# Starting the up projection on the first token half, and normalizing the second half without its weights

## The chip, the cores and the metric

One core of a Trainium2 chip runs the whole layer in one launch. The metric is the device time of that launch in microseconds, and lower is better. Before the change the median of three runs is 1382.29 us.

## The reference, cut to what matters

The layer takes 1024 tokens of width 1024. It mixes chunked attention with a gated convolution, then closes with a layer norm, and the result feeds a feed-forward block with a width of 2816 per branch:

```python
    mix = (g_att * y_att + g_conv * y_conv) @ w_o[l]
    x = layer_norm(ALPHA * x + mix, ln1_g[l], ln1_b[l])
    ffn = conv_ffn(x, w_up[l], ffn_conv_w[l], ffn_conv_b[l], w_down[l])
    x = layer_norm(ALPHA * x + ffn, ln2_g[l], ln2_b[l])

def conv_ffn(x, w_up, w_dw, b_dw, w_down):
    u = x @ w_up
    a, b = jnp.split(u, 2, axis=-1)
    a = causal_dwconv(a, w_dw, b_dw)
    return (jax.nn.gelu(a) * b) @ w_down

def layer_norm(x, g, b):
    ...
    y = xc * lax.rsqrt(var + LN_EPS) * g.astype(jnp.float32) + b.astype(jnp.float32)
```

The change sits between the first layer norm and the first products of `x @ w_up`.

## The kernel before, in words

**Precision.** Every float32 operand of a product is split into a high and a low part (`hi` by a copy on ScalarE, `lo` by a subtraction on VectorE), and each product takes three matmuls, high-high, high-low and low-high.

**The up projection.** It runs as 22 "quads". A quad computes two strips of 128 output features for all 1024 tokens. Tokens are split into two halves of 512 and the contraction into two halves of 512, and a Strassen-like form with seven products in place of eight is used. Each product is 4 x 3 matmuls of 128x512. The token side of the seven products are the forms `xf[1]` to `xf[7]`: forms 1 and 2 are the two contraction halves of the first 512 tokens, and forms 3 to 7 all need the second 512 tokens (form 4 is one block of them, 5, 6, 7 and 3 are differences and sums). The weight side: `wr` holds three raw blocks of a quad, for products 1, 3 and 2; `w13` serves products 5 and 7, and `w24` products 6 and 4, from sums that GpSimd makes (`prep_sums`, L809 to L812) into the tile `wt`. `parts_of` (L797, L798) splits weights; `product` (L821 to L823) issues the matmuls.

**What comes ahead of the quads.** The products with `w_o` (`mm3`, L196 to L198) give the sum that the layer norm closes, for token tiles 0 to 3 first and then 4 to 7. `close_tile` normalizes one tile of 128 tokens: `take` (L687) adds a bank to the residual with the sum accumulated, `norm` (L692 to L706) squares on ScalarE, makes the reciprocal root with a handful of small VectorE instructions, and applies weights and biases of the norm along the row with two VectorE instructions of 128x1024 (L705, L706). `turn0` transposes the first token half on TensorE (L745) and makes forms 1 and 2; `turn1` (L770 to L778) does so for the second half and makes forms 4, 5, 7, 6 and 3, all five for each of the four blocks `i`. In `turn1` forms 6 and 3 are computed by GpSimd (L773, L774). The normalized rows are also written to memory (`x1_d`, L858 and L872), since the last layer norm needs them again.

**Order.** The program is traced in the order of the code. A scheduler with a cost model then sets the order on each engine, by priority in program order among what it reckons ready; so the instructions of one engine can stand in another order than in the code, but each engine runs its own list in order. SBUF is laid out by the kernel's own `Arena`, which prefers places that were freed long ago; a tile in a place freed late waits for the last readers of what lay there.

**PSUM.** Eight banks: two `mm`, one `tp`, one `pv`, two pairs `s`. A quad uses `oa` and `od` (two `mm`, or `tp` and `pv`) and a pair for `oc` and `ob`.

Of the kernel before, what the change touches and what calls it, by code (L numbers as in the profile page):

```python
# [14 lines left out]
P = 128  # L15
T = 1024
# [25 lines left out]
C_FB = C_FW + FT * FTAPS  # L42
NPAR = C_FB + FT

# [71 lines left out]
def build(ctx, tc, xT, x, w_v, w_in, w_ao, w_co, w_o, w_up, w_dn, par, rel, rows, out):  # L116
# [561 lines left out]
    def close_tile(t, scale, g_bc, b_bc, out=None):  # L678
# [81 lines left out]

    def turn1():

        for n in (4, 5, 7, 6, 3):
            part(n)
        for i in range(4):
            o = bank2()
            turned(o[:, 0], 1, i + 4)
            turned(o[:, 1], 1, i)
            x22, x5, x7, x6, x3 = (sb(f"xs{n}_{i}", [P, HT]) for n in (4, 5, 7, 6, 3))
            S.activation(x22, o[:, 0], AF.Copy)  # L770
            V.tensor_sub(x5, o[:, 1], x22)
            V.tensor_sub(x7, xs[1][i], o[:, 1])
            G.tensor_sub(x6, x5, xs[1][i])  # L773
            G.tensor_add(x3, x6, xs[2][i])  # L774
            for n, a in ((4, x22), (5, x5), (7, x7), (6, x6), (3, x3)):
                hi, lo = xf[n][i]
                S.activation(hi, a, AF.Copy)  # L777
                V.tensor_sub(lo, a, f32(hi))  # L778
            sb.free(x22, x5, x7, x6, x3)
        sb.free(*xs[1], *xs[2])  # L780
# [18 lines left out]

    def prep_raw(q):  # L800

        if q < 2 * FP:
            parts_of(wr, quads[q][:, 1:4])

# [51 lines left out]
    x1_d = [tc.dram_tile([P, D], F32, name=f"x1_d{t}") for t in range(8)]  # L856
    for t in range(4):
        nc.sync.dma_start(x1_d[t], res[t])  # L858
        sb.free(res[t])
    for a in wo + mix[1]:  # L860
        sb.free(*a)
    sb.free(g_bc, b_bc)
    wt.append(sb("wt", [P, 4, HT]))
    w13 = pair_of_parts("w13", 2)
    w24 = pair_of_parts("w24", 2)
    prep_sums(0)
    parts_of(w13, wt[0][:, 0:2])
    parts_of(w24, wt[0][:, 2:4])
    turn1()
    quad_r.append(sb("quad1", [P, 4, HT]))  # L870
    for t in range(4, 8):
        nc.sync.dma_start(x1_d[t], res[t])  # L872
        sb.free(res[t])

    a_r = Ring("a", 2, [P, 2 + T])
    for t in a_r.t:
        G.memset(t[:, 0:2], 0.0)
    y_r = Ring("y", 4, [P, T])
    tmp = {n: sb(f"u{n}", [P, HT]) for n in ("1", "3", "U", "e", "21", "12", "22", "5", "6", "7", "8")}
# [3 lines left out]
    def quad(q, take11, dst21, dst12, dst22, over=None):  # L883

        if q % 2 == 0:
            oa, od = bank(), bank()
# [5 lines left out]
        done = over or (lambda n: None)  # L892
        product(oa, wr, 0, 1, True)
        done(1)
        S.activation(tmp["1"], oa, AF.Copy)
        product(od, wr, 1, 3, True)
        done(3)
        S.activation(tmp["3"], od, AF.Copy)
        product(oa, wr, 2, 2, False)
        done(2)  # L900
        take11(oa)
# [9 lines left out]
        done(6)  # L911
        V.tensor_add(tmp["U"], tmp["1"], ob)  # L912
        V.tensor_sub(dst12, od, tmp["U"])
# [89 lines left out]

    load_quad()
    for j in range(FP):
        f2 = (j, j + FP)
        a2 = [a_r(), a_r()]
        y2 = [y_r(), y_r()]
        quad(2 * j, lambda o: S.activation(a2[0][:, 2:2 + HT], o, AF.Copy), a2[0][:, 2 + HT:], a2[1][:, 2:2 + HT],
             a2[1][:, 2 + HT:])  # L1010
        for f, a, y in zip(f2, a2, y2):
# [11 lines left out]
        quad(2 * j + 1, lambda o: V.tensor_mul(y0[:, h0], y0[:, h0], o), tmp["21"], tmp["12"], tmp["22"],  # L1023
             over if j == FP - 1 else None)
        V.tensor_mul(y1[:, h0], y1[:, h0], tmp["12"])
# [98 lines left out]
def _layout(inputs):  # L1124
# [9 lines left out]
    def cols(v):  # L1134
# [48 lines left out]
```

## Time and profile before

| | |
|---|---|
| median of 3 runs (lowest to highest) | 1382.29 us (1380.49 to 1383.54) |
| the profiled execution's own time | 1380.95 us |
| its span in the profile | 1379.2 us |
| TensorE busy | 1334.7 us (97%) |
| VectorE busy | 977.7 us (71%) |
| ScalarE busy | 605.6 us (44%) |
| GpSimd busy | 350.6 us (25%) |

The 1.75 us between the span and the profiled execution's time lie outside the span. Busy TensorE says that a matmul was in flight, at either of its two clock levels, and not that it went at its peak; so the table alone doesn't tell how much of the span is lost.

### The profile page before, as it was taken

What the parts mean: (1) busy time and instruction counts of PE and PEld (TensorE: products, weight loads), DVE (VectorE), ACT (ScalarE), POOL (GpSimd) and SP (SyncE); (2) the same over time, 40 slices, a digit from 0 to 9 for tenths busy, and PEclk for the clock granted to TensorE, in tenths of its full rate; (3) what the DMA queues carried; (4) which work ended last, traced back from release to release, by engine and by line L of the source; (5) the groups of instructions that cost most, each with busy time, mean ns of one, the idle gap of its engine ahead of it and who ended that gap; (6) DMA issues with size and microseconds to landing.
All of it is one profiled execution on the core that took longest, in us unless ns stands there. A gap on an engine that the chain in (4) does not pass through costs nothing.

```text
span 1379.2 us, 16028 instructions
## 1 busy us (share of the span) xinstructions
PE 1334.7 (97%) x6004; PEld 1082.0 (78%) x6004; DVE 977.7 (71%) x1399; ACT 605.6 (44%) x916; POOL 350.6 (25%) x247
## 2 busy tenths in 40 slices
PE   9999999999999999999959999999999999998996
PEld 8877887887888888888737888888888878777885
DVE  5278888887799935746596565566666558997668
ACT  4346555656661137322453433334333444443453
POOL 1000000000000000000055566565555546972000
PEclk9999999999999999999969999999999999999999
DMA  7011111112101111621123323332223247753323
GB/s 268 16 46 41 40 56 41 56 51 82 47 31 46 55 37 52 223 92 51 45 62 107 108 87 115 115 115 89 103 96 103 100 173 267 263 166 93 92 84 123
DMA packets 48495, 132.29 MB, mean 96 GB/s; under 512 B 5393, under 2 KB 5529, under 8 KB 45601
## 3 DMA queue, kind: packets, MB, share of 16 engines
q1 hardware_dynamic: 48416, 131.26, 27.8%
q8 instruction: 47, 0.77, 0.2%
q14 instruction: 32, 0.25, 0.1%
HBM read 101.07 MB, written 30.17 MB: 95 GB/s over the span
## 4 chain that ended last, share of the span: by engine, by line
PE 82%; DVE 9%; ACT 3%; POOL 3%; issue 2%; DMA 1%; POOLq 0%; DVEq 0%; SPq 0%; ACTq 0%
PE mm L196 6%; PE mm L197 6%; PE mm L198 6%; PE s L196 5%; PE s L197 5%; PE s L198 5%; PE s L821 4%; PE s L822 4%; PE s L823 4%; PE mm L822 2%; PE mm L823 2%; PE mm L821 2%; PE s L1051 2%; PE s L1052 2%; PE tp L456 2%; PE s L1050 2%
## 5 line engine op out<-in xcount | busy, mean ns | idle before, releaser
L196 PE MATMUL mm<-xh,whi 128*128 128x512 f32 x384 | 157.9, 411 | 2.0 <-ACT qq L266 2.0
L414 DVE SCALAR_TENSOR_TENSOR acc<-hpad,par,acc 128x1024 f32<-128x1024 f32 x120 | 152.3, 1278 | 0.7
L198 PE MATMUL mm<-xh,wlo 128*128 128x512 f32 x384 | 151.8, 395 | 0.0
L197 PE MATMUL mm<-xl,whi 128*128 128x512 f32 x384 | 151.5, 395 | 0.0
L809 POOL TENSOR_TENSOR wt<-quad 128x512 f32<-128x512 f32 x22 | 28.3, 1288 | 467.7 <-ACT junk L696 375.9
L180 ACT ACTIVATE whi<-wraw 128x1024 fp32r<-128x1024 f32 x40 | 42.4, 1060 | 109.3 <-PE s L197 65.8
L798 DVE TENSOR_TENSOR wrl<-quad,wrh 128x1536 fp32r<-128x1536 f32 x22 | 42.7, 1942 | 60.8 <-ACT wrh L797 60.8
L198 PEld LDWEIGHTS mm<-xh,wlo 128*128 128x128 f32 x384 | 72.2, 188 | 15.1
L958 POOL TENSOR_TENSOR dn<-dn,dn 128x512 f32<-128x512 f32 x44 | 73.7, 1697 | 32.7 <-DMA actr<-act_d 14.7
L196 PEld LDWEIGHTS mm<-xh,whi 128*128 128x128 f32 x384 | 72.4, 189 | 11.9 <-ACT qq L266 2.9
L197 PEld LDWEIGHTS mm<-xl,whi 128*128 128x128 f32 x384 | 72.7, 189 | 9.2
L821 PE MATMUL s<-xfh,w24h 128*128 128x512 f32 x176 | 73.5, 418 | 2.1 <-DVE uU L912 1.9
L822 PE MATMUL s<-xfh,w24l 128*128 128x512 f32 x176 | 68.8, 391 | 0.0
L823 PE MATMUL s<-xfl,w24h 128*128 128x512 f32 x176 | 68.8, 391 | 0.0
L458 ACT ACTIVATE pth<-tp 128x512 fp32r<-128x512 f32 (+3 forms) x96 | 41.5, 433 | 54.1 <-PE tp L456 53.5
L181 DVE TENSOR_TENSOR wlo<-wraw,whi 128x1024 fp32r<-128x1024 f32 x40 | 48.7, 1219 | 23.0 <-ACT whi L180 22.8
L459 DVE TENSOR_TENSOR ptl<-tp,pth 128x512 fp32r<-128x512 f32 (+3 forms) x96 | 46.8, 488 | 18.5 <-ACT pth L458 17.9
L1014 DVE SCALAR_TENSOR_TENSOR y<-a,par,y 128x1024 f32<-128x1024 f32 x22 | 38.6, 1756 | 29.3 <-ACT y L1013 29.3
L439 ACT ACTIVATE p<-p,st 128x640 f32<-128x640 f32 (+2 forms) x64 | 44.4, 694 | 28.6 <-DVE st L437 28.0
L821 PE MATMUL mm<-xfh,wrh 128*128 128x512 f32 x132 | 52.8, 400 | 3.1 <-ACT xfh L777 3.1
L1013 ACT ACTIVATE y<-a,par 128x1024 f32<-128x1024 f32 x22 | 27.4, 1245 | 62.4 <-POOL a L914 57.5
L812 POOL TENSOR_TENSOR wt<-wt,quad 128x512 f32<-128x512 f32 x22 | 54.1, 2458 | 0.9
(567 smaller groups left out, 3842.2 us busy)
## 6 DMA issues: line engine op xcount, KB each, us to landing
quad<-in_w_up SPq DMA_DIRECT2D x22, 1024.0 KB, 5.2
actr<-act_d SPq DMA_DIRECT2D x77, 256.0 KB, 2.7
wraw<-in_w_in SPq DMA_DIRECT2D x32, 512.0 KB, 3.5
act_d<-u SPq DMA_DIRECT2D x44, 256.0 KB, 2.0
dn<-in_w_dn SPq DMA_DIRECT2D x44, 256.0 KB, 4.0
act_d<-y SPq DMA_DIRECT2D x33, 256.0 KB, 2.3
res<-in_x SPq DMA_DIRECT2D x8, 512.0 KB, 5.8
wraw<-in_w_o SPq DMA_DIRECT2D x8, 512.0 KB, 3.5
```

The lines of the kernel that those rows point to most:

```text
L181: V.tensor_sub(lo, raws[i], f32(hi))
L196: PE.matmul(o, ah, bh, start=first, stop=False)
L197: PE.matmul(o, ah, bl, start=False, stop=False)
L198: PE.matmul(o, al, bh, start=False, stop=last)
L414: V.scalar_tensor_tensor(a, hp[:, j:j + T], col(C_CW + c * TAPS + j), a, op0=OP.mult, op1=OP.add)
L439: S.activation(pt, pt, AF.Exp, bias=st[:, 0:1], scale=-1.0, accum_out=st[:, 1:2])
L459: last_lo[0] = V.tensor_sub(pl[:, :w], o[:, :w], f32(ph)[:, :w])
L812: G.tensor_add(t[:, 3], t[:, 2], b[:, 3])
L821: PE.matmul(o, wh, xh, start=go, stop=False, skip_group_check=not first)
L822: PE.matmul(o, wl, xh, start=False, stop=False, skip_group_check=not first)
L823: PE.matmul(o, wh, xl, start=False, stop=i == 3, skip_group_check=not first)
L958: G.tensor_add(dn[j][d], dn[j][d], dn[j][b])
```

## The change

The up projection's first two quads get a code path of their own, and the layer norm of the second token half is split.

- `close_plain` takes the place of `close_tile` for tiles 4 to 7. Mean and variance come from `bn_stats` and `bn_aggr` on VectorE, and ScalarE writes the normalized row without weights in one instruction. Weights and biases of the norm come in at the eviction of the transposed block in `turn1`, where they lie along partitions and so are a scale and a bias of the ScalarE copy (two more groups of columns, `C_G1` and `C_B1`, in the table of parameters). The weighted row that the end of the layer needs is made apart, by `rest` (two VectorE instructions and one write).
- Products 1 and 2 of both first quads are issued ahead of `turn1`. The second quad has raw weights of its own (`wr1`), and its load stands ahead of `turn1`.
- `turn1` makes form 4 for all blocks, then 7, 5, 6 and 3, each for all four blocks, all on VectorE; `quad_first` runs the rest of the first quad in the order of 4, 7, 5, 6, 3.
- `prep_sums(0)`, the writes of tiles 0 to 3 and the `wt` tile move ahead of tile 6 in the code.

```diff
+    def close_plain(t):
+        r, st = res[t], st_r()
+        v, y, z = (st[:, i:i + 1] for i in range(13, 16))
+        def take(o, c):
+            rc = r[:, cols[c]]
+            V.scalar_tensor_tensor(rc, rc, ALPHA, o, op0=OP.mult, op1=OP.add)
+            V.bn_stats(st[:, 6 * c:6 * c + 6], rc)
+        def norm():
+            V.bn_aggr(st[:, 12:14], st[:, 0:12])
+            S.activation(y, v, AF.Sqrt, bias=eps)
+            V.tensor_scalar(v, v, EPS, None, op0=OP.add)
+            V.reciprocal(y, y)
+            V.scalar_tensor_tensor(z, v, y, y, op0=OP.mult, op1=OP.mult)
+            V.tensor_scalar(z, z, -0.5, 1.5, op0=OP.mult, op1=OP.add)
+            V.tensor_mul(y, y, z)
+            V.scalar_tensor_tensor(z, st[:, 12:13], -1.0, y, op0=OP.mult, op1=OP.mult)
+            S.activation(r, r, AF.Identity, bias=z, scale=y)
+        def rest():
+            a = sb(f"x1r{t}", [P, D])
+            V.tensor_mul(a, r, g_bc)
+            V.tensor_add(a, a, b_bc)
+            nc.sync.dma_start(x1_d[t], a)
+            sb.free(a)
+        return take, norm, rest
...
+    def turn1(after):
+        def parts(n, i, a):
+            hi, lo = sb(f"xfh{n}{i}", [P, HT], F32R), sb(f"xfl{n}{i}", [P, HT], F32R)
+            xf.setdefault(n, []).append((hi, lo))
+            S.activation(hi, a, AF.Copy)
+            V.tensor_sub(lo, a, f32(hi))
...
         for i in range(4):
             o = bank2()
-            turned(o[:, 0], 1, i + 4)
-            turned(o[:, 1], 1, i)
-            x22, x5, x7, x6, x3 = (sb(f"xs{n}_{i}", [P, HT]) for n in (4, 5, 7, 6, 3))
-            S.activation(x22, o[:, 0], AF.Copy)
-            V.tensor_sub(x5, o[:, 1], x22)
-            V.tensor_sub(x7, xs[1][i], o[:, 1])
-            G.tensor_sub(x6, x5, xs[1][i])
-            G.tensor_add(x3, x6, xs[2][i])
-            for n, a in ((4, x22), (5, x5), (7, x7), (6, x6), (3, x3)):
-                hi, lo = xf[n][i]
-                S.activation(hi, a, AF.Copy)
-                V.tensor_sub(lo, a, f32(hi))
+            for a, b, k in ((a22[i], o[:, 0], i + 4), (a21[i], o[:, 1], i)):
+                turned(b, 1, k)
+                S.activation(a, b, AF.Identity, bias=col(C_B1 + k), scale=col(C_G1 + k))
+            parts(4, i, a22[i])
+        after()
+        for i in range(4):
+            a7 = sb(f"xs7{i}", [P, HT])
+            V.tensor_sub(a7, xs[1][i], a21[i])
+            parts(7, i, a7)
...
+        for i in range(4):
+            V.tensor_sub(a21[i], a21[i], a22[i])
+            parts(5, i, a21[i])
...
+        for i in range(4):
+            V.tensor_sub(a21[i], a21[i], xs[1][i])
+            parts(6, i, a21[i])
+        for i in range(4):
+            V.tensor_add(a21[i], a21[i], xs[2][i])
+            parts(3, i, a21[i])
...
+    rests = []
     for t in range(4, 8):
-        take, norm = close_tile(t, ALPHA, g_bc, b_bc)
+        take, norm, rest = close_plain(t)
...
         norm()
+        rests.append(rest)
...
         if t == 5:
             turn0()
+            for i in range(4):
+                nc.sync.dma_start(x1_d[i], res[i])
+                sb.free(res[i])
+            wt.append(sb("wt", [P, 4, HT]))
+            prep_sums(0)
+        if t > 4:
+            rests.pop(0)()
     for a in wo + mix[1]:
         sb.free(*a)
+    quad_r.append(sb("quad1", [P, 4, HT]))
+    load_quad()
+    w24 = pair_of_parts("w24", 2)
+    parts_of(w24, wt[0][:, 2:4])
     w13 = pair_of_parts("w13", 2)
     parts_of(w13, wt[0][:, 0:2])
-    turn1()
+    wr1 = pair_of_parts("wr1", 3)
+    prep_raw(1, wr1)
+    tmp = {n: sb(f"u{n}", [P, HT]) for n in ("1", "1b")}
+    oa = [bank(), bank()]
+    for o, w, u in ((oa[0], wr, "1"), (oa[1], wr1, "1b")):
+        product(o, w, 0, 1, True)
+        S.activation(tmp[u], o, AF.Copy)
+        product(o, w, 2, 2, False)
+
+    def after():
+        prep_sums(1)
+        rests.pop(0)()
+        for t in range(4, 8):
+            sb.free(res[t])
+        sb.free(g_bc, b_bc)
+
+    turn1(after)
...
+    def quad_first(take11, dst21, dst12, dst22):
+        od, cb = ps_t.tile([P, HT], F32, tag="tp", name="tp"), bank2()
+        oc, ob = cb[:, 0], cb[:, 1]
+        take11(oa[0])
+        product(oc, w24, 1, 4, True)
+        S.activation(tmp["3"], oc, AF.Copy)
+        product(oc, w13, 1, 7, False)
+        product(od, w13, 0, 5, True)
+        V.tensor_add(tmp["e"], tmp["3"], od)
+        parts_of(w13, wt[0][:, 0:2])
+        product(ob, w24, 0, 6, True)
+        V.tensor_add(tmp["U"], tmp["1"], ob)
+        V.tensor_add(dst21, tmp["U"], oc)
+        G.tensor_sub(dst22, tmp["e"], dst21)
+        parts_of(w24, wt[0][:, 2:4])
+        product(od, wr, 1, 3, False)
+        V.tensor_sub(dst12, od, tmp["U"])
```

The second quad runs in `quad` with its products 1 and 2 left out, since they are begun already, and with `wr1` in place of `wr`. All later quads are as before.

## Rows read from the trace of the kernel before

**Rows 1.** Windows over the hand-over: length, busy time of each engine, granted clock.

```profile
682.00:685.42 3.42, 3.42 (x17) 2.77 (x16) 1.98 (x7) 1.54 (x3) 0.00 (x0) 1.00 0.00 0
...
696.59:722.79 26.20, 20.10 (x62) 13.35 (x62) 25.36 (x29) 14.62 (x25) 11.64 (x9) 0.61 0.18 59
722.79:757.76 34.97, 31.55 (x129) 23.85 (x130) 21.88 (x19) 13.78 (x14) 19.73 (x13) 1.00 0.31 101
...
779.00:1000.00 221.00, 221.00 (x960) 178.20 (x959) 134.55 (x127) 83.06 (x86) 128.07 (x81) 1.00 0.29 103
```

**Rows 2.** Timeline of TensorE: start, duration, line, tiles, idle before and releaser.

```profile
685.42 0.60 PE L745 MATMUL s<-ident,res 128*128 128x128 f32 x4
685.77 0.48 PE L821 MATMUL mm<-xfh,wrh 128*128 128x512 f32 x1
...
696.59 2.40 PE L745 MATMUL s<-ident,res 128*128 128x128 f32 x10 [7.35 <-DVE res L706]
...
724.32 0.40 PE L822 MATMUL mm<-xfh,w13l 128*128 128x512 f32 x1
...
729.31 0.39 PE L823 MATMUL s<-xfl,w24h 128*128 128x512 f32 x1
```

**Rows 3.** Timeline of VectorE over the close of tile 7 and `turn1`.

```profile
656.61 0.14 DVE L700 TENSOR_SCALAR st<-st 128x1 f32<-128x1 f32 x1
...
657.50 1.28 DVE L706 SCALAR_TENSOR_TENSOR res<-res,st,b 128x1024 f32<-128x1024 f32 x1
...
686.00 0.67 DVE L687 SCALAR_TENSOR_TENSOR res<-res,pv 128x512 f32<-128x512 f32 x1
...
716.57 0.68 DVE L771 TENSOR_TENSOR xs<-s,xs 128x512 f32<-128x512 f32 x1
717.17 0.67 DVE L772 TENSOR_TENSOR xs<-xs,s 128x512 f32<-128x512 f32 x1
717.76 4.97 DVE L778 TENSOR_TENSOR xfl<-xs,xfh 128x512 fp32r<-128x512 f32 x5
```

**Rows 4.** Timeline of GpSimd in the same stretch.

```profile
688.48 1.27 POOL L809 TENSOR_TENSOR wt<-quad 128x512 f32<-128x512 f32 x1 [375.92 <-ACT junk L696]
...
717.39 1.29 POOL L773 TENSOR_TENSOR xs<-xs,xs 128x512 f32<-128x512 f32 x1 [3.10 <-ACT u L895]
718.76 1.62 POOL L774 TENSOR_TENSOR xs<-xs,xs 128x512 f32<-128x512 f32 x1
...
727.13 1.30 POOL L809 TENSOR_TENSOR wt<-quad 128x512 f32<-128x512 f32 x1 [4.23 <-DMA quad<-in_w_up]
```

**Rows 5.** Waits of the DMA queue: who waited for whom, total, times, longest.

```profile
SPq L790 <- DVE xfl L778: 25.3, 1, 25.3
```

**Rows 6.** Groups of instructions by line: busy us, mean ns.

```profile
L664 DVE TENSOR_TENSOR t<-t,t 128x1024 f32<-128x1024 f32 x8 | 9.8, 1221 | 0.1
L798 DVE TENSOR_TENSOR wrl<-quad,wrh 128x1536 fp32r<-128x1536 f32 x22 | 42.7, 1942 | 60.8 <-ACT wrh L797 60.8
L443 DVE TENSOR_SCALAR p<-p,st 128x512 f32<-128x512 f32 x8 | 3.9, 483 | 0.1
L1013 ACT ACTIVATE y<-a,par 128x1024 f32<-128x1024 f32 x22 | 27.4, 1245 | 62.4 <-POOL a L914 57.5 <-ACT u L895 2.8 <-DVE a L917 2.0
L797 ACT ACTIVATE w13h<-wt 128x1024 fp32r<-128x1024 f32 x22 | 23.3, 1060 | 56.2 <-PE s L823 53.1 <-POOL wt L810 3.1
L777 ACT ACTIVATE xfh<-xs 128x512 fp32r<-128x512 f32 x20 | 12.0, 626 | 6.7 <-POOL xs L774 2.6 <-POOL xs L773 2.3 <-DVE xs L771 1.7
L699 ACT ACTIVATE st<-st,eps 128x1 f32<-128x1 f32 x16 | 4.5, 290 | 2.5 <-DVE st L698 2.5
```

**Rows 7.** DMA issues by line: size, median us to landing.

```profile
quad<-in_w_up SPq DMA_DIRECT2D x22, 1024.0 KB, 5.2
...
x_d<-res SPq DMA_DIRECT2D x8, 512.0 KB, 2.6
```

More of the change, by code (lines that the diff above doesn't have):

```diff
@@ L42 @@
 C_FB = C_FW + FT * FTAPS
-NPAR = C_FB + FT
+C_G1 = C_FB + FT
+C_B1 = C_G1 + KD
+NPAR = C_B1 + KD
 FP = FT // 2
@@ L759, in turn0 @@
             S.activation(xs[n][i], tp, AF.Copy)
[L761 to L764 removed]
+    def turn1(after):
[4 more added lines that the diff above has]
+            V.tensor_sub(lo, a, f32(hi))
+        a22 = [sb(f"xs4{i}", [P, HT]) for i in range(4)]
+        a21 = [sb(f"xs5{i}", [P, HT]) for i in range(4)]
         for i in range(4):
             o = bank2()
[L767 to L779 removed]
+            for a, b, k in ((a22[i], o[:, 0], i + 4), (a21[i], o[:, 1], i)):
[7 more added lines that the diff above has]
+            parts(7, i, a7)
+            sb.free(a7)
+        for i in range(4):
+            V.tensor_sub(a21[i], a21[i], a22[i])
+            parts(5, i, a21[i])
+            sb.free(a22[i])
+        for i in range(4):
[4 more added lines that the diff above has]
+            parts(3, i, a21[i])
+            sb.free(a21[i])
         sb.free(*xs[1], *xs[2])
@@ L798, in parts_of, with prep_raw @@
         V.tensor_sub(lo, src, f32(hi))
-    def prep_raw(q):
+    def prep_raw(q, dst=None):
         if q < 2 * FP:
-            parts_of(wr, quads[q][:, 1:4])
+            parts_of(dst or wr, quads[q][:, 1:4])
     def prep_sums(q):
@@ L836, in build @@
     close_tiles((2, 3, 0, 1), lambda t: o8[2 * t:2 * t + 2], ALPHA, g_bc, b_bc)
+    x1_d = [tc.dram_tile([P, D], F32, name=f"x1_d{t}") for t in range(8)]
+    rests = []
     for t in range(4, 8):
-        take, norm = close_tile(t, ALPHA, g_bc, b_bc)
+        take, norm, rest = close_plain(t)
         for c in range(2):
@@ L877, in build, with quad @@
         G.memset(t[:, 0:2], 0.0)
-    y_r = Ring("y", 4, [P, T])
-    tmp = {n: sb(f"u{n}", [P, HT]) for n in ("1", "3", "U", "e", "21", "12", "22", "5", "6", "7", "8")}
+    y_r = Ring("y", 2, [P, T])
+    for n in ("3", "U", "e", "21", "12", "22"):
+        tmp[n] = sb(f"u{n}", [P, HT])
     act_d = [{n: tc.dram_tile([P, HT], F32, name=f"act_d{n}_{j}") for n in range(1, 8)} for j in range(FP)]
     h0, h1 = cols
-    def quad(q, take11, dst21, dst12, dst22, over=None):
-        if q % 2 == 0:
+    def quad_first(take11, dst21, dst12, dst22):
[15 more added lines that the diff above has]
+        V.tensor_sub(dst12, od, tmp["U"])
+    def quad(q, take11, dst21, dst12, dst22, over=None, begun=None):
+        wr_, one = (wr, "1") if begun is None else (wr1, "1b")
+        if begun is not None:
+            oa, od = begun, ps_v.tile([P, HT], F32, tag="pv", name="pv")
+        elif q % 2 == 0:
             oa, od = bank(), bank()
@@ L892, in quad @@
         done = over or (lambda n: None)
[L893 to L896, printed above, removed]
+        if begun is None:
+            product(oa, wr, 0, 1, True)
+            done(1)
+            S.activation(tmp["1"], oa, AF.Copy)
+        product(od, wr_, 1, 3, True)
         done(3)
         S.activation(tmp["3"], od, AF.Copy)
-        product(oa, wr, 2, 2, False)
-        done(2)
+        if begun is None:
+            product(oa, wr, 2, 2, False)
+            done(2)
         take11(oa)
@@ L911, in quad @@
         done(6)
-        V.tensor_add(tmp["U"], tmp["1"], ob)
+        V.tensor_add(tmp["U"], tmp[one], ob)
         V.tensor_sub(dst12, od, tmp["U"])
@@ L1008, in build @@
         y2 = [y_r(), y_r()]
-        quad(2 * j, lambda o: S.activation(a2[0][:, 2:2 + HT], o, AF.Copy), a2[0][:, 2 + HT:], a2[1][:, 2:2 + HT],
-             a2[1][:, 2 + HT:])
+        first = [lambda o: S.activation(a2[0][:, 2:2 + HT], o, AF.Copy), a2[0][:, 2 + HT:], a2[1][:, 2:2 + HT],
+                 a2[1][:, 2 + HT:]]
+        if j:
+            quad(2 * j, *first)
+        else:
+            quad_first(*first)
         for f, a, y in zip(f2, a2, y2):
@@ L1023, in build @@
         quad(2 * j + 1, lambda o: V.tensor_mul(y0[:, h0], y0[:, h0], o), tmp["21"], tmp["12"], tmp["22"],
-             over if j == FP - 1 else None)
+             over if j == FP - 1 else None, None if j else oa[1])
+        if j == 0:
+            sb.free(*wr1, tmp.pop("1b"))
+            for n in ("5", "6", "7", "8"):
+                tmp[n] = sb(f"u{n}", [P, HT])
+            y_r.t += [sb(f"y{i}", [P, T]) for i in (2, 3)]
+            y_r.i = 2
         V.tensor_mul(y1[:, h0], y1[:, h0], tmp["12"])
```

16 lines of the change are left out of this document (1 added, 15 removed).

## The prediction

> **What bounds the kernel now.** I read the windows first, then each engine's timeline inside the stretch that they single out, then the waits of the DMA queue. TensorE is busy without a gap up to 685.42 us and again from 757.76 us on, at the full clock [rows 1]; what is hidden there costs nothing, and what ends the stretch between sooner ends the kernel sooner. The reader is to see that in these 72.34 us TensorE has little to do. One matmul of 128x512 follows the next by (729.31 - 724.32)/22 = 0.227 us [rows 2]. By the code the stretch holds the first two quads (2 x 7 x 12 = 168 matmuls), 8 matmuls of the third and the 32 transposes of the second token half; four transposes take 685.77 - 685.42 = 0.35 us [rows 2]. That is 176 x 0.227 + 8 x 0.35 = 42.8 us of work: 29.5 us are lost.
>
> Where? After 722.79 us TensorE does 129 matmuls, 29.3 us of work, in 34.97 us [rows 1]: 5.7 us lost. So 23.8 us are lost before. There it first stands idle for 7.35 us until the last normalized tile is there [rows 2]; then, from 696.59 to 722.79 us, VectorE is busy for 25.36 of 26.20 us while TensorE nibbles at a clock of 0.61 [rows 1]. VectorE makes five forms per block there, each block takes about 6 us (two differences, then five low parts [rows 3]), and every product waits for its form of the last block. So two things set the length: when the normalized second half arrives, and VectorE's work on the forms; and what TensorE still has to do once the forms are all there.
>
> **What it adds and removes on VectorE.** I add up VectorE from 685.42 us to the last form.
> - Close of tile 7: one take at 0.67 [rows 3]; one `bn_stats` of 128x512, which the trace doesn't show: between 0.48 us (a one-input instruction of that shape [rows 6]) and 0.67 (the take), and I take 0.67, a pass over float32 with a reduction being nearer the take; the small ones: five took 657.50 - 656.61 = 0.89 us [rows 3], two more are 0.4. Sum 2.6. The two passes over 128x1024 (1.28 each where GpSimd is still [rows 3]) leave the path.
> - `rest` of tiles 6 and 7: four of 128x1024 at 1.22 [rows 6], 4.9. Those of tiles 4 and 5 fall where VectorE idles (busy 1.98 of 3.42 us and less ahead of it [rows 1]) and cost nothing; on the path they would be 4.9 more.
> - Low parts of `w24` and `w13`, 2 x 1.22, and of `wr1`, 1.94 [rows 6]: 4.4.
> - `turn1`: 4 low parts for form 4 and 4 x 4 x 2 for the others, 36 instructions. Starts lie 0.60 us apart where GpSimd is still (717.17 - 716.57 [rows 3]): 21.6.
> - GpSimd beside it. Five low parts take 4.97 us [rows 3] where 5 x 0.60 = 3.0 would do, while GpSimd works 2.9 us on forms 6 and 3 [rows 4]: 2.0 us lost per 2.9. The change moves those forms to VectorE (in the 36 already), and leaves only `prep_sums(1)` beside it, 4 x 1.28 = 5.1 us [rows 4]: 3.5.
> - Evictions of the first quad (three, 0.60 each) and new low parts of `w13` and `w24` (2.4) fall in between: 4.2.
>
> Sum 41.2: the last form is there at 726.6 us if VectorE never waits. It waits for the tile-7 chain a little: 685.42 + 0.67 + 0.67 + 0.2, root 0.29, small ones 1.1, ScalarE's pass 1.25 with a scale and a bias per partition [rows 6], some 0.5 us of hand-overs, 690.1; one of the two weight copies of 1.06 [rows 6] in ScalarE's list ahead of it makes it 691. I put 1.5 us for it: 728 us. That is later than the 722.79 of now, so no form comes sooner at the end of the list. The gain lies in what is left to do then.
>
> The Trainium skill, SBUF — State Buffer, section "Who interferes with whom", says that a VectorE instruction with two SBUF inputs and a GpSimd instruction that reads SBUF lock each other out wholly. The rows show 2.0 us lost per 2.9, not 2.9. By that rule `prep_sums(1)` would cost 5.1 in place of 3.5 us, and the time would be 1.6 us longer.
>
> **What TensorE has left.** Before the last form it can do products 1, 2, 4, 7, 5 and 6 of the first quad and three quarters of 3, and 1, 2, 7 and half of 6 of the second: 72 + 9 + 42 = 123 matmuls, 27.9 us, and 2.8 of transposes, in 42.6 us. 36 of them (product 2 of the first quad, 1 and 2 of the second) are new cover for the idle 7.35 us. Product 1 of the first quad ran there already [rows 2]. `w13` of the second quad can only be split behind product 5, `w24` behind product 6, so the second quad's 6, 4, 5 and 3 can't all come sooner. After it: 3 + 12 + 12 + 12 + 6 = 45, and 8 of the third quad, 53 x 0.227 = 12.0 us. Of the 5.7 us that were lost there before, some go: the second quad's load was issued only at the end of `turn1`, when the queue had waited 25.3 us for the place [rows 5], and its sums began at 727.13 us on landing [rows 4]; now it is loaded ahead. But the third quad's `wr` can only be split behind product 3, and VectorE carries the convolution of the first pair in less time; I put 4 us. End 728 + 16 = 744 us, against 757.76: 13.8 us saved.
>
> **What lies beside other work.** `prep_sums(0)` waited until 688.48 us for a place in SBUF [rows 4]; now it runs under the matmuls with `w_o`. The ScalarE evictions in `turn1` with scale and bias cost at most (1.25 - 1.06)/2 = 0.1 us more than copies [rows 6]; eight of them and four copies, 12 x 0.63 [rows 6] + 8 x 0.1 = 8.4 us, and VectorE has `wr1`, `rest` and form 7 of the first blocks to do meanwhile. Without that cover the last form would be 3 to 4 us later. Three more kinds of instructions in SyncE's list (writes of tiles 0 to 3 and 4 to 6, moved ahead of the second quad's load) hold it only if their rows are late (below). The 16 columns more in the parameters are nothing.
>
> From 13.8 us I take 2 for an order by a cost model that will not fit: an engine's list that stands as the model reckoned leaves a wait wherever a transfer or another engine comes later than reckoned. **12 us saved**: the profiled execution's 1380.95 becomes 1369; its runs' median lies 1.3 us above it, so I predict 1370 us.
>
> **Rivals.**
> - *TensorE at the low level (chance 0.19).* Between 696.59 and 722.79 us the granted clock was 0.61, mostly 1.2 GHz, after 7.35 us of idleness [rows 1, 2]; a matmul at half the clock is 0.227 x 2 = 0.45 us, a product 5.4. If the new, still sparse, products keep that level from 696 to 722 us, five products and the transposes take 5 x 5.4 + 5.6 = 33 us, more than the 26 from 696 to 722, and the second quad's 7 and 6 (18 matmuls, 4.1 us) and 2 to 3 us of the first's fall behind the last form: 5 to 7 us saved, 1376 us. Against: 36 matmuls more fill the first gap. The Trainium skill, TensorE: Matmul & The Clock Gate, Part 1, says the same of the cause, that the slow level is what an idle TensorE falls back to.
> - *TensorE is fed to the full (0.12).* VectorE's evictions and splits are put behind the forms, the last form comes at 724 us, and only products 3 and 5 of the second quad are left: 35 matmuls, 8 us, and 2 us of waits, 734 us: 24 saved, some 1359 us.
> - *The second quad's load is late (0.24, other side from a point on).* Its products 1 and 2 stand in the code ahead of the transposes. A load takes 5.2 us [rows 7], its split 1.5 and 1.9 us, the two products 5.4 and a copy between 0.9: landing at 691 us starts the transposes at 700 if the list keeps the code's order, landing at 697 starts them at 706. Each us past 691 is one us of the saving: 12 us are gone at 703, and from 706 on the kernel is slower by over 2.8 us. The load's place is one that the rows of tile 6 (`rest`, written by the same queue) or the last `w_o` products leave; one read until 690 us with a write of 2.6 us [rows 7] behind it lands at 697.8, 1386 us. For it: this very load waited 25.3 us for a place before [rows 5]. Against: the scheduler would have to reckon the load earlier than it is, or it puts the transposes first. I give 0.14 to slower, 0.10 to within 2.8 us.
> - *The forecast (0.45)*: 7 to 18 us saved.
>
> **How the numbers follow.** 0.2% is 2.8 us, about what a measurement can tell from no change. Faster: 0.45 + 0.19 + 0.12 = 0.76; same 0.10; slower 0.14. The likeliest's own range is 1364 to 1375 us. The range for 8 in 10 goes from 1361 (most of the second rival beyond it) to 1386 (the late load at 697 us just inside).
>
> **What would show it.** TensorE without the 7.35 us gap: some 48 matmuls with `wr` and `wr1` between 685 and 700 us. The transposes of the second half beginning at 690 to 693 us, no GpSimd instruction on the forms, the last low part of form 3 at 724 to 730 us, later than now. Continuous matmuls from about 744 us on in place of 757.76. Wrong would be: transposes after 700 us, a wait of a product for `wr1`, of ScalarE for a place in SBUF, or a temporary of the first quad that lies where form 3 is read last, which would hold product 7 until the forms are done.

## The result and the profile after

The changed kernel takes 1365.92 us (median of 4 runs, 1363.76 to 1366.44) against 1381.39 for the kernel before on the same chip (1380.48 to 1383.54): a ratio of 0.988, 95% interval 0.9869 to 0.9892. The prediction was 1370 us with 1364 to 1375 for the likeliest case alone. The profiled execution took 1366.28 us with a span of 1364.5 (before 1379.2).

The windows of the kernel after, cut at the last matmul with `w_o` (684.98 us), the last product ahead of the last transposes, the first `w24` product, the last form and the 181st matmul of a product, against [rows 1]; columns as there:

```profile
684.98:691.18 6.20, 6.18 (x29) 4.91 (x28) 5.55 (x19) 2.35 (x5) 5.09 (x4) 1.00 0.00 0
691.18:700.58 9.40, 6.57 (x30) 4.25 (x29) 8.32 (x10) 8.86 (x13) 0.00 (x0) 0.75 0.28 113
700.58:723.11 22.53, 21.45 (x85) 16.26 (x86) 21.26 (x35) 14.30 (x23) 1.33 (x3) 0.95 0.13 48
723.11:743.38 20.27, 17.96 (x73) 14.12 (x71) 18.25 (x17) 9.51 (x9) 12.64 (x8) 0.92 0.23 78
743.38:1000.00 256.62, 256.62 (x1113) 206.62 (x1112) 154.01 (x147) 96.95 (x101) 148.95 (x94) 1.00 0.30 104
```

The last form (the low part that is ready last) comes at 723.11 us, no sooner than the 722.73 of before [rows 3]. But TensorE has done 25 + 85 = 110 products' matmuls by then, where before it had done 47, and from 743.38 to 1000 us it never waits. The third window shows how: 85 matmuls in 22.53 us at a clock of 0.95 while VectorE works on the forms; before, 62 TensorE instructions in 26.20 us at 0.61.

TensorE's timeline after, where [rows 2] had one wait of 7.35 us:

```profile
684.75 0.39 PE L200 MATMUL pv<-woh,mxl 128*128 128x512 f32 x1
684.97 0.39 PE L868 MATMUL mm<-xfh,wrh 128*128 128x512 f32 x1
...
691.18 0.39 PE L870 MATMUL mm<-xfl,wrh 128*128 128x512 f32 x1
692.37 0.44 PE L777 MATMUL s<-ident,res 128*128 128x128 f32 x2 [0.79 <-ACT res L733]
693.50 0.44 PE L777 MATMUL s<-ident,res 128*128 128x128 f32 x2 [0.69 <-ACT res L733]
694.70 1.37 PE L777 MATMUL s<-ident,res 128*128 128x128 f32 x8 [0.76 <-ACT xs L808]
696.55 3.95 PE L777 MATMUL s<-ident,res 128*128 128x128 f32 x16 [0.49 <-ACT xs L808]
700.58 0.80 PE L868 MATMUL s<-xfh,w24h 128*128 128x512 f32 x1
...
742.22 0.39 PE L870 MATMUL s<-xfl,w24h 128*128 128x512 f32 x1
```

Products 1 and 2 of the first quad cover the close of tile 7; the transposes of the last tiles begin at 692.37 in place of 696.59. The last row shown is the 176th matmul of a product; in the kernel before, the 176th starts at 757.54 us. VectorE's timeline over the same close, and at the end of the forms, against [rows 3]:

```profile
685.96 0.68 DVE L721 SCALAR_TENSOR_TENSOR res<-res,pv 128x512 f32<-128x512 f32 x1
686.56 1.28 DVE L722 BATCH_NORM_STATS2 st<-res 128x6 f32<-128x512 f32 x2
687.76 0.33 DVE L725 BATCH_NORM_AGGREGATE st<-st 128x2 f32<-128x12 f32 x2
...
689.44 1.27 DVE L729 SCALAR_TENSOR_TENSOR st<-st 128x1 f32<-128x1 f32 x1
...
691.13 0.16 DVE L732 SCALAR_TENSOR_TENSOR st<-st 128x1 f32<-128x1 f32 x1
...
721.82 1.29 DVE L800 TENSOR_TENSOR xfl<-xs,xfh 128x512 fp32r<-128x512 f32 x2
723.02 0.69 DVE L960 TENSOR_TENSOR uU<-u,s 128x512 f32<-128x512 f32 x1
...
730.79 2.83 DVE L845 TENSOR_TENSOR wrl<-quad,wrh 128x1536 fp32r<-128x1536 f32 x1
```

GpSimd after, against [rows 4]: it makes no form any more, and the second quad's sums come before the forms rather than behind them.

```profile
685.53 1.30 POOL L856 TENSOR_TENSOR wt<-quad 128x512 f32<-128x512 f32 x1 [70.74 <-DVE w13l L845]
...
689.40 1.30 POOL L859 TENSOR_TENSOR wt<-wt,quad 128x512 f32<-128x512 f32 x1
...
727.51 2.27 POOL L858 TENSOR_TENSOR wt<-wt,quad 128x512 f32<-128x512 f32 x1
729.86 2.14 POOL L859 TENSOR_TENSOR wt<-wt,quad 128x512 f32<-128x512 f32 x1
```

And TensorE's waits over the whole kernel after (what waited for what, total, times, longest):

```profile
PE s L1149 <- DVE hl1wl L1062: 6.1, 1, 6.1
PE mm L869 <- DVE wrl L845: 2.3, 1, 2.3
...
PE mm L1148 <- ACT hl4ah L1063: 1.7, 1, 1.7
```

So the span's 14.7 us divide in three. From the start to the last `w_o` matmul 0.4 us were saved (685.18 to 684.75). From there to the last Up product 16.5: 462.0 us before, 445.5 after. From the last Up product to the end 2.2 were given back: 232.0 before, 234.2 after. The give-back can be read in the down stage: VectorE's list holds eleven additions to the residual, released by GpSimd, ahead of `hl1wl`. TensorE asks for `hl1wl` from 1235.24 us on, 17.0 us sooner than before (1252.27), but the additions start at 1231.12, only 14.8 sooner (1245.93); the difference is 2.2 us, and the wait grows from 3.91 to 6.12 us. First the two waits of TensorE in the kernel before that bear on these stretches (in the down stage and in the up projection) and its additions, then the kernel after:

```profile
PE s L1051 <- DVE hl1wl L973: 4.3, 2, 3.9
```

```profile
1124.51 0.50 PE L821 MATMUL s<-xfh,w24h 128*128 128x512 f32 x1 [1.20 <-DVE uU L912]
```

```profile
1245.93 9.98 DVE L1088 SCALAR_TENSOR_TENSOR resb<-resb,p 128x512 f32<-128x512 f32 x11 [1.19 <-POOL p L1093]
```

```profile
1231.12 9.98 DVE L1186 SCALAR_TENSOR_TENSOR resb<-resb,p 128x512 f32<-128x512 f32 x11 [1.19 <-POOL p L1191]
1241.02 0.68 DVE L1062 TENSOR_TENSOR hl1wl<-dn,hl1wh 128x512 fp32r<-128x512 f32 x1
```

### The profile page after: what moved, and what is told of

Its sections match the earlier page's. It is cut to its first block, busy times and chain, and to the rows that moved or that the text cites. A ratio compares the mean times of both kernels' runs of the same rounds, so it can differ in the third digit from the quotient of the medians.

```text
span 1364.5 us, 16008 instructions
## 1 busy us (share of the span) xinstructions
PE 1330.8 (98%) x6004; PEld 1082.1 (79%) x6004; DVE 977.9 (72%) x1399; ACT 608.4 (45%) x916; POOL 334.9 (25%) x239
## 4 chain that ended last, share of the span: by engine, by line
PE 86%; DVE 9%; ACT 3%; issue 1%; DMA 1%; POOL 0%; POOLq 0%; DVEq 0%; ACTq 0%; SPq 0%
PE mm L198 6%; PE mm L199 6%; PE mm L200 6%; PE s L198 5%; PE s L200 5%; PE s L199 5%; PE s L868 5%; PE s L870 4%; PE s L869 4%; PE mm L869 3%; PE mm L870 3%; PE mm L868 3%; PE s L1149 2%; PE s L1150 2%; PE s L1148 2%; PE tp L458 2%
## 5 line engine op out<-in xcount | busy, mean ns | idle before, releaser
L869 PE MATMUL mm<-xfh,wrl 128*128 128x512 f32 x128 | 50.6, 395 | 2.3 <-DVE wrl L845 2.3
L844 ACT ACTIVATE w24h<-wt 128x1024 fp32r<-128x1024 f32 x22 | 23.4, 1062 | 62.9 <-PE s L870 62.9
```

Of the source, the lines that this page charges most:

```text
L869: PE.matmul(o, wl, xh, start=False, stop=False, skip_group_check=not first)
```

## The experiments

All times are medians. "Up" is the stretch from the start of the last `w_o` matmul to the last Up product, "last form" the end of the last low part counted from that same `w_o` matmul's end, "ready" the matmuls of products done by then, "rest" what follows the last Up product. The same changed program run twice (`after`, `again`) differs by 0.06 us in the median, but by 1.1 us in Up of its one profiled execution, so Up alone settles nothing below some 1.5 us. The runs come from several chips; the median of before lay between 1381.30 and 1382.56 us beside them.

> The changed kernel once more, for a comparison on the same chip as the next three: 1364 to 1367 us by every theory; it says how far medians of one program lie apart.

| kernel | median us (range) | ratio to before, 95% | last form | ready | Up | rest |
|---|---|---|---|---|---|---|
| before | 1381.39 (1380.48–1383.54) | | 37.3 | 47 | 462.0 | 232.0 |
| after | 1365.92 (1363.76–1366.44) | 0.9869–0.9892 | 38.1 | 110 | 445.5 | 234.2 |
| again | 1365.98 (1365.64–1366.46) | 0.9869–0.9896 | 37.2 | 110 | 444.4 | 235.2 |
| held | 1367.96 (1367.92–1368.77) | 0.9885–0.9911 | 36.3 | 77 | 446.9 | 234.3 |
| weighted | 1374.69 (1374.44–1376.33) | 0.9935–0.9959 | 38.1 | 109 | 450.7 | 237.8 |
| norm_alone | 1371.44 (1370.05–1372.09) | 0.9906–0.9933 | 32.5 | 37 | 455.2 | 230.7 |
| gpsimd_forms | 1372.61 (1371.51–1373.49) | 0.9919–0.9943 | 40.2 | 96 | 451.1 | 234.2 |
| by_block | 1364.26 (1364.18–1365.62) | 0.9859–0.9885 | 44.0 | 128 | 445.0 | 233.2 |
| more_vector | 1368.00 (1367.67–1368.20) | 0.9883–0.9910 | 39.6 | 110 | 446.8 | 235.1 |
| no_rest | 1367.25 (1365.32–1369.63) | 0.9884–0.9914 | 35.7 | 107 | 449.0 | 231.9 |
| late_load | 1368.18 (1367.27–1369.14) | 0.9891–0.9924 | 40.7 | 110 | 446.5 | 234.8 |
| code_place | 1364.34 (1363.82–1366.38) | 0.9865–0.9895 | 36.9 | 110 | 444.0 | 234.4 |
| split_wr | 1362.29 (1361.65–1365.50) | 0.9852–0.9882 | 37.3 | 116 | 443.0 | 235.7 |
| split_wr_place | 1363.17 (1361.75–1364.08) | 0.9848–0.9875 | 36.7 | 116 | 441.0 | 236.4 |

**held: the begun products held back.** Product 2 of the first quad and 1 and 2 of the second are tied to the end of form 6 by a one-column write.

```diff
     turn1(after)
+    prep_raw(1, wr1)
+    S.activation(tmp["1"], oa[0], AF.Copy)
+    product(oa[0], wr, 2, 2, False)
+    product(oa[1], wr1, 0, 1, True)
...
             parts(6, i, a21[i])
+            if i == 3:
+                S.activation(tmp["1"][:, 0:1], a21[i][:, 0:1], AF.Copy)
+                S.activation(wr1[0][:, 0, 0:1], a21[i][:, 0:1], AF.Copy)
```

> The changed kernel, but the 36 matmuls newly begun early (product 2 of the first quad, products 1 and 2 of the second) are held: the copy and the weights that they need wait for the last block of form 6. Theory: these 36 x 0.227 = 8.2 us filled time in which TensorE had nothing else, so held they come on top behind the forms: 6 to 9 us slower than the changed kernel (about 1373 us). Rival: VectorE sets the end of the stretch and TensorE finds room for them anyway: 0 to 2 us slower.

The median rose by 2.0 us, for 36 matmuls (36 x 0.227 = 8.2 us) that are no longer begun early. The gap is back: 4.0 us ahead of the transposes. (In the kernel after only 13 of the 36 lay in that gap; the other 23 ran from 702.79 to 709 us, while VectorE made the forms.) The windows of this kernel show where it is made good, 77 matmuls before the last form and then 105 TensorE instructions in 24 us without a wait, while VectorE catches up behind them:

```profile
697.00:721.40 24.40, 20.39 (x81) 14.65 (x82) 23.93 (x38) 19.09 (x32) 0.21 (x2) 0.92 0.10 40
721.40:745.40 24.00, 24.00 (x105) 19.32 (x104) 18.68 (x18) 10.23 (x10) 13.22 (x8) 1.00 0.36 120
```

In the kernel after, TensorE runs out of prepared weights at that place and waits; here it has products in store instead. Beginning early is worth 2 us, not 8: the run fits its rival.

**weighted: tiles 4 to 7 normalized with their weights, as before.** The evictions of the transposed tiles become copies again, the rows are written as they are.

```diff
-        take, norm, rest = close_plain(t)
+        take, norm = close_tile(t, ALPHA, g_bc, b_bc)
+        rest = lambda t=t: nc.sync.dma_start(x1_d[t], res[t])
...
-                S.activation(a, b, AF.Identity, bias=col(C_B1 + k), scale=col(C_G1 + k))
+                S.activation(a, b, AF.Copy)
```

> The changed kernel with the old close of tiles 4 to 7: weights and biases of the norm applied along the row on VectorE, plain copies at the transposed eviction, no separate weighted row. Theory: VectorE does the same number of long passes, but they stand again ahead of the transposes; the second half comes some 4 us later, and the forms with it: 2 to 4 us slower. Rival: the early products cover the wait and the unweighted norm buys nothing: within 1 us.

8.8 us slower in the median, 5.2 of them in Up and 3.6 behind it. The last form is not later (38.1 us) and 109 matmuls are ready, but the stretch behind the forms now holds these TensorE waits (window 684 to 760 us):

```profile
PE s L868 <- DVE ue L997: 2.9, 1, 2.9
PE mm L868 <- ACT wr1h L844: 2.2, 1, 2.2
PE s L868 <- ACT w13h L844: 2.1, 1, 2.1
```

So the place where I had put the gain, an earlier chain, is not where it shows: the planner's list is another one, and the loss falls on weights and evictions that come late. Nor does the count of matmuls ready say what a kernel loses: held is 33 short and 2.0 us slower, this one is 1 short and 8.8 us slower. In the down stage a wait of 6.8 us for `hl2wh` appears.

**norm_alone: this one part put into the kernel before.** Its rows of tiles 4 to 7 go on to the second residual without weights, so the passes that `rest` would cost are left out.

```diff
-        take, norm = close_tile(t, ALPHA, g_bc, b_bc)
+        take, norm = close_plain(t)
...
-            S.activation(x22, o[:, 0], AF.Copy)
-            V.tensor_sub(x5, o[:, 1], x22)
-            V.tensor_sub(x7, xs[1][i], o[:, 1])
+            x21 = sb(f"x21_{i}", [P, HT])
+            S.activation(x22, o[:, 0], AF.Identity, bias=col(C_B1 + i + 4), scale=col(C_G1 + i + 4))
+            S.activation(x21, o[:, 1], AF.Identity, bias=col(C_B1 + i), scale=col(C_G1 + i))
+            V.tensor_sub(x5, x21, x22)
+            V.tensor_sub(x7, xs[1][i], x21)
```

> The kernel before with one part of the change alone: tiles 4 to 7 are closed by bn_stats and a ScalarE pass without the weights, which come in at the ScalarE evictions of the transposed tiles (the rows of these tiles that go on to the second residual are left without weights). Products, quads, loads and the GpSimd forms stay as before. Theory, the parts add up: the first transposes 4 to 5 us sooner (692 in place of 696.6), every form after them too, and the last Up product 4 to 6 us sooner, 1375 to 1377 us. Rival, the parts need each other, as the second quad's load still waits for the forms' place: below 2 us. Rival, this part is nearly all of the gain, since the early products were worth only 2 us: 9 us or more, below 1372 us.

11.1 us faster than before in the median on the same chip, ratio 0.9906 to 0.9933. In the traces the span is 8.9 us shorter: 0.8 up to the last `w_o` matmul, 6.8 in Up, 1.3 behind it. TensorE's timeline: the transposes begin 7.3 us sooner, but then it waits for each block's forms as before, since GpSimd and the five forms of a block are unchanged:

```profile
689.28 1.31 PE L770 MATMUL s<-ident,res 128*128 128x128 f32 x10 [0.64 <-ACT res L733]
691.58 1.09 PE L770 MATMUL s<-ident,res 128*128 128x128 f32 x8 [0.99 <-ACT x L797]
696.36 0.80 PE L849 MATMUL mm<-xfh,wrh 128*128 128x512 f32 x1 [3.69 <-ACT xfh L805]
...
702.72 0.80 PE L849 MATMUL mm<-xfh,wrh 128*128 128x512 f32 x1 [3.00 <-ACT xfh L805]
```

So where nothing covers the chain behind the last `w_o` matmul, its length is worth some 7 us: a little over what the sum of parts says. The median asks for more, 11 us, as if this part were most of the gain. Of the 2.2 us between the two, 1.6 come from before (its traced execution took 1380.95 us, its median beside norm_alone was 1382.56), and 0.6 from norm_alone, whose traced execution lay that much above its median. It is an upper bound for the part, since the weights of the rows have to be put on somewhere.

**gpsimd_forms: forms 6 and 3 back on GpSimd.**

```diff
-            V.tensor_sub(a21[i], a21[i], xs[1][i])
+            G.tensor_sub(a21[i], a21[i], xs[1][i])
...
-            V.tensor_add(a21[i], a21[i], xs[2][i])
+            G.tensor_add(a21[i], a21[i], xs[2][i])
```

> The changed kernel, but the differences and sums of forms 6 and 3 are made by GpSimd again. Theory by the price read before (2.0 us lost on VectorE per 2.9 us of GpSimd): 8 x 0.60 = 4.8 us leave VectorE, and 8 x 1.28 = 10.2 us of GpSimd beside it cost 7 us: 2 to 4 us slower. Rival: a relief of the fullest engine: 2 to 5 us faster.

6.7 us slower, 5.6 of them in Up. Eight instructions on GpSimd take 1.67 to 1.70 us each, and the VectorE instructions beside them start 1.7 us apart in place of 0.60 (first VectorE, then GpSimd):

```profile
711.37 14.29 DVE L800 TENSOR_TENSOR xfl<-xs,xfh 128x512 fp32r<-128x512 f32 x11
```

```profile
712.14 5.01 POOL L821 TENSOR_TENSOR xs<-xs,xs 128x512 f32<-128x512 f32 x3 [1.21 <-DVE xfl L800]
717.12 6.78 POOL L824 TENSOR_TENSOR xs<-xs,xs 128x512 f32<-128x512 f32 x4
```

VectorE had 8 x 0.6 = 4.8 us less to do, but eight of its instructions lost 1.09 us each, 8.7 us together where I had reckoned 7, and the last form is 2.1 us later. Only 96 matmuls are ready, and at 718.35 us TensorE had to wait 3.4 us for an eviction of the first quad. Moving these forms to VectorE was right, and worth more than the contention alone that I had read in [rows 3, 4].

**by_block: the forms block after block, not form after form** (the four loops, of 7, 5, 6 and 3, become one).

```diff
-        for i in range(4):
-            V.tensor_sub(a21[i], a21[i], a22[i])
-            parts(5, i, a21[i])
-            sb.free(a22[i])
-        for i in range(4):
-            V.tensor_sub(a21[i], a21[i], xs[1][i])
-            parts(6, i, a21[i])
+            V.tensor_sub(a21[i], a21[i], a22[i])
+            parts(5, i, a21[i])
+            sb.free(a22[i])
+            V.tensor_sub(a21[i], a21[i], xs[1][i])
+            parts(6, i, a21[i])
...
```

> The changed kernel, but the forms 7, 5, 6 and 3 are made block by block and not form by form; same instructions. Theory: the gain lies in what is left to do once the last form is there; by blocks every product of the first quad waits for the last block, the second quad's w13 and w24 can only be split behind that, and some 20 matmuls more are left: 4 to 8 us slower. Rival: only VectorE's sum counts, which is the same: within 1 us.

No slower: 1364.26 us. The last form comes 5.9 us later (44.0), but 128 matmuls are ready by then. The order of use is not what gains; my theory fell, and the rival, that only VectorE's sum counts, fits.

**more_vector: VectorE 2.4 us longer.**

```diff
             V.tensor_sub(lo, a, f32(hi))
+            if n == 6:
+                V.tensor_sub(lo, a, f32(hi))
```

> The four low parts of form 6 are computed twice, the second time into the same place: 4 x 0.6 = 2.4 us more of VectorE ahead of the last form and nothing else. Theory, VectorE's sum up to the last form sets when the steady part begins: the last low part of form 3 at some 725.5 us in place of 723.1, and the last Up product 2.0 to 2.6 us later, 1368 us. Rival, it is what TensorE has left that sets the end, and TensorE can fill 2.4 us of VectorE with products that it has in store: 0 to 0.8 us later.

2.0 us slower than the same program run beside it (again), the ranges apart. Behind the last form the stretch is that of again, 2.0 us later: `wrl` begins at 731.81 in place of 729.81, and TensorE's wait of 2.3 us for it ends at 734.7 in place of 732.7. So in this order VectorE's sum does set the end of the hand-over. The run moves the last form and `wrl` together and can't tell which of them does it; by_block, where the last form came 5.9 us later at no loss, says that it is not the last form by itself.

**no_rest: the rows of tiles 6 and 7 written without their weights.**

```diff
+            if t > 5:
+                nc.sync.dma_start(x1_d[t], r)
+                return
             a = sb(f"x1r{t}", [P, D])
```

> The changed kernel, but the weighted rows of tiles 6 and 7 are left out: the rows are written without the weights and biases of the norm, four VectorE passes of 1.22 us less. Theory: VectorE's sum sets when the last form comes: 3 to 5 us faster. Rival: in that stretch ScalarE's evictions set it (VectorE only fills gaps with these passes): 0 to 1 us faster.

4.9 us less for VectorE, and no gain: the median is 1.3 us higher, with ranges that overlap. The traced execution, the slowest of the four, is 3.5 us longer in Up. The planner made another list: products 1 and 2 of the second quad ahead of most transposes, and VectorE idle:

```profile
695.83 0.39 PE L873 MATMUL mm<-xfl,wr1h 128*128 128x512 f32 x1
696.06 0.27 PE L780 MATMUL s<-ident,res 128*128 128x128 f32 x1
697.10 0.55 PE L780 MATMUL s<-ident,res 128*128 128x128 f32 x3 [0.77 <-ACT res L733]
...
700.45 1.03 PE L780 MATMUL s<-ident,res 128*128 128x128 f32 x8
```

```profile
699.47 1.29 DVE L803 TENSOR_TENSOR xfl<-xs,xfh 128x512 fp32r<-128x512 f32 x2 [4.18 <-ACT xfh L802]
```

This doesn't measure what the rows cost. It shows a list like that of my third rival (products ahead of the transposes) with a load that is in time: counted from the last `w_o` matmul, the transposes end 3.9 us later than in the kernel after. The last form still comes 2.5 us sooner; what was won there goes behind it, where TensorE waits 6.0 us in place of 2.3, above all for the third quad's raw weights.

**late_load: the second quad's load behind the close of tile 7.**

```diff
     quad_r.append(sb("quad1", [P, 4, HT]))
+    G.tensor_copy(quad_r[1][:, 0, 0:1], res[7][:, 0:1])
     load_quad()
```

> The changed kernel, but the second quad's load must wait until the tile-7 row is normalized (one element of it is first copied into the load's place), so that it lands at about 698 us in place of about 685. The prediction's rival: each us past 691 is a us of loss because the products stand ahead of the transposes: about 7 us slower. Theory now: the scheduler puts the transposes first, and the low parts of wr1 were made at 699 us anyway: 0 to 2 us slower.

2.2 us slower. The load was issued at 693.06 us, and its high parts came at 699.54 (ScalarE), 14.8 us later than in the kernel after (684.76). The planner put the transposes first, and only the first `wr1` product waited:

```profile
701.08 0.80 PE L868 MATMUL mm<-xfh,wr1h 128*128 128x512 f32 x1 [3.06 <-ACT wr1h L844]
701.75 0.79 PE L868 MATMUL s<-xfh,w24h 128*128 128x512 f32 x1
```

What it did cost can be read in VectorE's list. The second quad's sums on GpSimd wait for the same load, so they now lie beside the low parts of `wr1` and of the forms, and the last form comes 2.6 us later:

```profile
701.05 2.69 DVE L845 TENSOR_TENSOR wr1l<-quad,wr1h 128x1536 fp32r<-128x1536 f32 x1 [2.07 <-ACT wr1h L844]
703.67 4.65 DVE L800 TENSOR_TENSOR xfl<-xs,xfh 128x512 fp32r<-128x512 f32 x4
```

At the rival's price, a microsecond for each past 691, a load that landed at 699.5 would have cost over 8. But the low parts of `wr1` were there at 703.7 us, 2.6 later than in the kernel after and not 14.8, since there they had stood behind `rest`; so the run gives no price per microsecond of lateness.

**code_place: the begun products written behind `turn1(after)` in the code.**

```diff
-    for o, w, u in ((oa[0], wr, "1"), (oa[1], wr1, "1b")):
-        product(o, w, 0, 1, True)
...
     turn1(after)
+    for o, w, u in ((oa[0], wr, "1"), (oa[1], wr1, "1b")):
+        product(o, w, 0, 1, True)
```

> The changed kernel, with the products 1 and 2 of the first two quads written behind the making of the forms in the code and not ahead of it; nothing else. Theory: the scheduler places by what it reckons ready, and what makes them early are the early weights and copies: within 1 us. Rival: the place in the code is what the change lives on: 6 to 9 us slower.

1364.34 us, its range overlapping that of after; 110 matmuls are ready in both. So the place in the code does next to nothing here, as the theory had it that the planner orders by when it reckons inputs ready.

**split_wr, split_wr_place: the third quad's raw weights split matrix by matrix**, so that product 1's low parts come first and not together with all three; then the same with code_place's edit.

```diff
-                parts_of(dst or wr, quads[q][:, 1:4])
+            if q == 2:
+                for i in (0, 2, 1):
+                    parts_of([a[:, i] for a in wr], quads[q][:, i + 1])
+            else:
+                parts_of(dst or wr, quads[q][:, 1:4])
```

> The changed kernel, but the raw weights of the third quad are split into high and low parts block by block (three pairs of instructions in place of one), block 0 first, so that product 1 of the third quad needs only the first pair. Theory: the changed kernel's one long wait after the forms, 2.3 us for these low parts, and the slower clock of the 6 matmuls behind it (6 x 0.2 us) go: 2 to 3.5 us faster. Rival: VectorE is full there, and the wait only moves to the next thing that it makes: within 1 us.

> The changed kernel with two edits at once: the third quad's raw weights split matrix by matrix (alone 2.5 us less up to the last Up product), and the begun products behind the transposes in the code (alone 1.5 us less, within what a measurement can tell). Theory, the third quad's low parts are what is late after the forms, and the place in the code does nothing: 1361 to 1364 us, as the split alone. Rival, both add: 1359 to 1361 us. Rival, the planner lays the list out anew and the split's gain goes: 1365 to 1368 us.

3.6 us faster than after in the median, though one of its four runs lies among those of after; with both edits 2.8 us faster than the same program run beside it, the ranges apart (1361.75 to 1364.08 against 1365.64 to 1366.46). The three pieces of 128x512 come one by one, behind the product of the first quad that uses the same place: the first is there at 691.6 us, where the whole of 128x1536 came at 733.6:

```profile
690.94 0.68 DVE L845 TENSOR_TENSOR wrl<-quad,wrh 128x512 fp32r<-128x512 f32 x1
...
725.94 1.58 DVE L845 TENSOR_TENSOR wrl<-quad,wrh 128x512 fp32r<-128x512 f32 x1
```

Product 1 of the third quad needs only the first piece, and nine of its matmuls are done by the last form (they are among the 116). The wait for `wrl` is gone and one of 2.6 us for `ue` at 734.4 takes its place, the next thing late on the same busy VectorE. With both edits Up is 4.5 us shorter than after, but 2.2 of it is given back behind Up, and the medians of the two versions can't be told apart: the second edit adds nothing that reaches the end. Either has a lower median than both kernels of the case.

## Why the prediction was right

The mechanism was right: no form comes sooner at the end, and the gain lies in what is left to do then. How much is left is not the whole of it: weighted has 109 matmuls ready, as good as the 110 of the kernel after, and is 5.2 us longer in Up, since operands come late behind the forms. That the number came close is in part luck, since several terms were off and their errors ran against each other. Point by point:

- **The cover.** Forecast: some 48 matmuls between 685 and 700 us. Measured: 25, all but one with `wr`, until 691.18, and none of the next nine microseconds, since `wr1`'s low parts were begun only at 699.41, behind `rest`. The 7.35 us gap went, as forecast, but this was the smaller part: held shows 2 us for all that was begun early.
- **The close of tile 7.** Forecast 691. Its last small instruction ended at 691.3, ScalarE's passes over tiles 6 and 7 at 693.4, and the transposes of tiles 6 and 7 began at 692.4 and 693.5. A `bn_stats` took 0.64 to 0.69 us (I took 0.67). But tile 6 closes in the same stretch, and GpSimd works beside the small ones; in norm_alone, with neither, the last small instruction ended at 687.9.
- **VectorE's sum, the term that was mis-sized.** Forecast 41.2 us and 1.5 of waiting; measured 5.55 + 8.32 + 21.26 = 35.1 us busy and 3.0 idle, the last form at 723.11 and not 728 (just outside the 724 to 730 that I had named as a sign). Three terms were too high. The sums of `prep_sums(1)` ran from 685.53 to 690.7 us beside the small instructions of the close, not beside the forms: about 1 us lost, not 3.5. Of the evictions and the new low parts of `w13` and `w24` (4.2 us) only one split of 1.2 us comes ahead of the last form; the rest is put behind it. Of the 2.4 us for the first `w24` and `w13` about 2 were over by 685. The second half of tile 6's close, some 2 us, I had left out. 41.2 - 2.5 - 3.0 - 1.9 + 2 = 35.8.
- **What TensorE had left.** Forecast 123 matmuls before the last form and 45 + 8 behind it; measured 110, and 66 up to the same 176th matmul. Forecast 12.0 us + 4 of waits, measured 66 x 0.227 = 15.0 us in 742.2 - 723.1 = 19.1, so 4.1 of waits: that term held, and its cause too, the third quad's `wr` (2.31 us, and six matmuls behind it 0.43 us apart). Forms 4.9 us sooner and 3.1 us more behind them: the 176th matmul starts at 742.2 where 744 was forecast, 757.5 before.
- **The allowance of 2 us for the planner's order** was not needed in Up, where the saving is 16.5 us, 1.6 more than at the 176th matmul; 1.2 of that is a wait for `uU` at 1124.51 us that only the kernel before has. It was taken in the down stage instead, which I hadn't looked at: 2.2 us, behind eleven additions in VectorE's list. 0.4 + 16.5 - 2.2 = 14.7, against 12. So 2 us were set aside for Up, which needed none, and about as much was lost where I had set nothing aside.
- **The low clock** didn't come: 0.95 from 700.58 to 723.11 us; only the stretch of the transposes stood at 0.75. **TensorE fed to the full** fell too: the last form came when that rival put it (724), but 66 matmuls were left, not 35. **The late load** wasn't late: issued at 679.95, split from 684.76. Had it been, its price would not have been that of the rival: late_load landed at 699.5 and lost 2.2 us.
- **The rule of the Trainium skill** that I weighed (SBUF — State Buffer, "Who interferes with whom") was put on `prep_sums(1)` beside the forms, and the kernel after has no such stretch. Elsewhere in its trace `wrl` took 2.83 us beside a GpSimd sum for its first 1.2 us, where `wr1l` took 1.75 alone: 1.1 us lost, nearer to the rule's full exclusion than the 2.0 per 2.9 of [rows 3, 4]. late_load has the stretch: beside the four sums `wr1l` took 2.69 us in place of 1.75 and four low parts 4.65 in place of 2.48 (at 709.45 us, without GpSimd). VectorE lost 3.1 us, near my 3.5 and not the 5.1 that I had drawn from the rule; but the sums themselves took 6.96 us in place of 5.17, so GpSimd lost 1.8 more, 4.9 us for both.

What the parts are worth: the norm without weights 5 us in Up taken out of the change and 7 put alone into before, the forms on VectorE 5.6, the begun products 2, the order of the forms nothing that shows. 5.2 + 5.6 + 2 = 12.8 of 16.5, though each was taken out by itself and such parts need not add up; what the earlier load and its place add was tried only as lateness (2.2 us), and the remainder is left open. Why GpSimd releases the residual's additions 14.8 us sooner in the down stage, and not 17, was not followed further; in both traces its sums just ahead of them wait for a load of `dn` (3.22 us before, 3.25 after).

## What to carry to other kernels

Where an engine that prepares operands stays the bound through a stage, ask not only when its last result comes, but what the other engine has left to do then and whether the operands of that are ready. Moving two VectorE passes per tile off the path to the transposes, taking GpSimd's work from beside that engine, or splitting its next large piece so that the first use comes first paid 3 to 9 us here, while beginning 36 matmuls early paid 2. Where a planner orders the instructions, an edit of one cost can remake the list (4.9 us less work for VectorE gained nothing), so a part's worth has to be measured inside the whole and alone. Follow a gain to the end of the kernel: 2.2 us of 16.9 went at the first place where a chain on other engines had not moved along.

## What the hardware showed that I had not expected

- A VectorE instruction on one element per partition took 1.27 us while GpSimd worked on 128x512 (689.44 us), where its like without GpSimd took 0.22 (norm_alone, and twice in late_load). It ended at 690.71 us, with the GpSimd instruction (690.70), and the rest of the normalization's small instructions stood behind it.
- GpSimd suffers as well: a sum of 128x512 took 1.30 us beside the small instructions and 2.27 beside VectorE's convolution (727.51). A form on GpSimd took 1.67 to 1.70 us in gpsimd_forms, beside a busy VectorE, where VectorE does one in 0.60.
- Two statistics instructions on 128x512 took 1.28 us, 0.64 each, as long as an addition over the same shape (0.68), and the aggregation of two tiles 0.33.
